# Held VectorE operations, and softmax weights turned on VectorE and through DRAM, in a one-layer hybrid decoder step

## The chip, the cores and the metric

The kernel runs on one core of a Trainium2 chip. The metric is the device time of one execution in microseconds; the time given is the median of three executions. The profile is of one further execution.

## The reference, cut to what matters

One decoder layer with three branches that read the same normalised input, for a prompt of 1024 tokens and for 8 sample tokens that share the weights:

```
h = rmsnorm(x);  q, k, v, gla_g, a_lr, u, pool_g, xq, xg, merge = split(h @ w_in)
br_gla  = rmsnorm(gla_chunked(q, k, v, log_sigmoid(a_lr @ w_a2 + b_a)/16, S0)) * silu(gla_g)
br_pool = multiscale_pool(u, hist) * silu(pool_g)
s = einsum('bthd,bmhd->bhtm', xq, mem_k) * 256 ** -0.5      # 4 heads of 256, 256 memory rows
c = einsum('bhtm,bmhd->bthd', softmax(s), mem_v)
br_x = c * silu(xg)
y = x + (sum over n of sigmoid(merge_n) * (branch_n @ w_branch_n)) @ w_out, then rmsnorm
```

The sample tokens run the same layer, each against its own cached memory keys and values. All is float32 (the matmuls in three products of split operands, see below), D_MODEL is 1024.

## The kernel before, in words

**Products.** The input projection is worked off in 36 `Pair`s of column blocks, each by a scheme of seven products instead of eight (`product`, `half`-wise). An operand is split into a high part, written by ScalarE, and a remainder, written by VectorE (`split`, L220 and L221; scaled, L223 and L224), and each product is three matmuls (`mm3`, L239 to L241): high by high, high by remainder, remainder by high. The operand sums of a pair (`of`, L300) are made by VectorE on the raw block that a DMA loaded; names are a11, a12, a22 (blocks) and s1 to s4 (sums, in the two `ws` tiles); the sums of product results are the `c` rows (L676, L693, L702) with the `r` that ScalarE saved (L611). Operands are prepared three products ahead.

**Side streams.** After each half product, `fill()` lets the other work advance, in amounts that constants and the costs yielded by each stream decide: the memory's keys and values, cross attention, GLA, pooling. TensorE, SyncE (SP) and the loads stand in written order. The order on VectorE, ScalarE and GpSimd is made by a scheduler; `tc.issue_after(x)` keeps an operation from standing earlier than x on its engine.

**Cross attention** (`cross_steps`). 4 heads by 4 chunks of 256 tokens make 16 steps. Step s runs scores(s), queries(s+1), the load of xq(s+2), a step of the sample tokens, values(s-2), another sample step, at the head's end the next head's memory, weights(s-1), and three more sample steps.

- `cross_scores`: 12 matmuls into a PSUM bank `pz`, maxima (nm, L766), exponentials (L75), reciprocal and scaling (L771, L773), giving p with tokens on partitions.
- `cross_weights`: four 128x128 transposes on TensorE (L781) into another `pz` bank, and the split of that bank into pTh and pTl.
- `cross_values`: 24 matmuls of the values by pT into `pz`, copied out to xo.
- `cross_sample`: for each head, 16 products with reduction on VectorE (L825, two for each of 8 sample tokens, of a key tile kc with a broadcast query qb) write the 16 columns of sc; two TensorE transposes (L835) read all of sc; then maxima (L837), the exponentials and the values.

There are two `pz` banks for all of this. Temporaries come from a ring of 14 tiles; key tiles from four others; qb from two tags of two buffers, which the gate's tiles use later. Queries, keys and pT are loaded by SP, which works in order.

**Elsewhere.** GLA's `states` scale and update the sample tokens' states, ScalarE and VectorE (L1098 on); `gate_work` stages the forget gate's loads and weights; `smask` is the mask that resets a scan (L979) every 64 tokens.

Of the kernel before, what the change touches and what calls it, by code (L numbers as in the profile page):

```python
# [18 lines left out]
P = 128  # L19
# [14 lines left out]
CT = 256  # L34
GATE = 16
NE = 30
NR = 14
WORK_A, WORK_B = 497.6, 108.0
WINDOWS = (2, 4, 8, 16)
HIST = 15  # L40
# [7 lines left out]
def trunk_kernel(ctx: ExitStack, tc: tile.TileContext,  # L48
# [81 lines left out]
    def Q(name):  # L130
        return wk.tile([P, QT], F32, tag="q", name=name, bufs=5)

    def tiny(w, name="t", bufs=8):
        return wk.tile([P, 16], F32, tag="t", name=name, bufs=bufs)[:, :w]


    ident = cp.tile([P, P], F32, name="ident")
    make_identity(nc, ident)

    smask = cp.tile([P, CT], BF16, name="smask")  # L140
    nc.gpsimd.memset(smask, 1.0)
    nc.gpsimd.memset(smask.rearrange("p (c t) -> p c t", t=64)[:, :, 0:1], 0.0)
    epst = cp.tile([P, 4], F32, name="epst")
    nc.gpsimd.memset(epst[:, 1:2], 1.0)
    nc.gpsimd.memset(epst[:, 2:3], -0.5 * math.log(DK))
# [38 lines left out]
    ssq = cp.tile([P, 16], F32, name="ssq")  # L184
    nc.vector.memset(ssq, 1.0)

    smp = cp.tile([P, 33 * NS], F32, name="smp")
    brs = [cp.tile([P, NK, NS], F32, name=f"brs{n}") for n in range(3)]
    als = cp.tile([P, NS], F32, name="als")
    als_parts = cp.tile([P, NS], F32R, name="alsp")  # L190
# [7 lines left out]

    PAIR = (P, 4, HT)
    xq_scr, v_scr = scratch(NH, "xqs", (NS, 256)), scratch(NH, "vs", (NS, 256))  # L200
    acc_scr = [scratch(NK, f"acc{n}_", (P, TT)) for n in range(2)]
    mkv_scr = [scratch(NH, f"mkvs{o}", (P, 2, DV)) for o in range(2)]
    al_scr = scratch(2, "als", (P, HT))
# [13 lines left out]
    def split(dst_hi, dst_lo, src, scale=None):  # L217

        if scale is None:
            last["hi"] = nc.scalar.activation(dst_hi, src, AF.Copy)  # L220
            last["lo"] = nc.vector.tensor_tensor(dst_lo, src, dst_hi.bitcast(F32), op=ALU.subtract)  # L221
        else:
            nc.scalar.activation(dst_hi, src, AF.Copy, scale=scale)  # L223
            nc.vector.scalar_tensor_tensor(dst_lo, src, scale, dst_hi.bitcast(F32), op0=ALU.mult, op1=ALU.subtract)  # L224

    def split_r(src, shape, name, scale=None):
        hi, lo = R(shape, F32R, name + "h"), R(shape, F32R, name + "l")
# [54 lines left out]
    class Pair:  # L282
# [11 lines left out]
        def operands(self):  # L294
            lo, hi = self.raw
            a11, a12, a21, a22 = lo[:, :, :P], hi[:, :, :P], lo[:, :, P:], hi[:, :, P:]

            def of(x, y, op, s=None):
                s = wk.tile([P, 4, P], F32, tag="ws", name="ws", bufs=2) if s is None else s
                nc.vector.tensor_tensor(s, x, y, op=op)  # L300
                return s

            def parts(src, name):
                h, l = W2(name + "h"), W2(name + "l")
                split(h, l, src)
                return h, l

            yield parts(a11, "a11")
            yield parts(a12, "a12")
            s1 = of(a21, a22, ALU.add)  # L310
            s2 = of(s1, a11, ALU.subtract)
            yield parts(s2, "s2")
            yield parts(s1, "s1")
            yield parts(of(a11, a21, ALU.subtract), "s3")
            yield parts(of(a12, s2, ALU.subtract, s2), "s4")
            yield parts(a22, "a22")
# [71 lines left out]
        return raw  # L388

    def W2S(dt):  # L390
        return wk.tile([P, 2, P], dt, tag="w2s", name="w2s", bufs=2)

    gate = {}

    def gate_loads():
        for i in range(2):
            gate["w", i] = W2S(F32)
            for j in range(8):
                nc.gpsimd.dma_start(out=gate["w", i][16 * j:16 * j + GATE],
                                    in_=w_a2[:, i * CT:(i + 1) * CT].rearrange("r (h n) -> r h n", h=2))  # L400
# [32 lines left out]
    def gate_work(n):  # L433
        if n == 1:
            gate_loads()
        elif n == 3:
            gate_inputs_load(0)
        elif n == 5:
            gate_weights()
        elif n == 8:  # L440
            gate_inputs(0)
        elif n == 10:
            gate_inputs_load(1)
        elif n == 12:
            gate_inputs(1)

    def mem_units():
# [309 lines left out]
    def cross_scores(h, c):  # L757
        xh, xl = cross["q", h, c]
        mh, ml = cross["mk", h]
        t = PZ()  # L760
        for j in range(2):
            for i in range(2):
                cs = slice(j * P, (j + 1) * P)
                mm3(t[:, j * NM:(j + 1) * NM], xh[:, i, cs], xl[:, i, cs], mh[:, i], ml[:, i], i == 0, i == 1)
        nm = tiny(2, "nm")
        nc.vector.tensor_reduce(nm, t.rearrange("p (j m) -> p j m", j=2), axis=AX.X, op=ALU.max, negate=True)  # L766
        p = R([2, NM], name="p")
        sm = tiny(2, "sm")
        for j in range(2):
            act(p[:, j], t[:, j * NM:(j + 1) * NM], AF.Exp, bias=nm[:, j:j + 1], accum_out=sm[:, j:j + 1])  # L770
        nc.vector.reciprocal(sm, sm)  # L771
        for j in range(2):
            nc.vector.tensor_scalar(p[:, j], p[:, j], sm[:, j:j + 1], None, op0=ALU.mult)  # L773
        cross["p", h, c] = p

    def cross_weights(h, c):
        p = cross["p", h, c]
        t = PZ()
        for a in range(2):
            for j in range(2):  # L780
                nc.tensor.transpose(t[:, (2 * a + j) * P:(2 * a + j + 1) * P], p[:, j, a * P:(a + 1) * P], ident)  # L781
        cross["pT", h, c] = split_r(t.rearrange("p (a t) -> p a t", a=2), [2, CT], "pT")

    def cross_values(h, c):
        ph, pl_ = cross["pT", h, c]
        vh, vl = cross["mv", h]
        g = R([2, CT], name="xo")
        t = PZ()
        for i in range(2):
            cs = slice(i * P, (i + 1) * P)  # L790
            for a in range(2):
                mm3(t[:, i * CT:(i + 1) * CT], vh[:, a, cs], vl[:, a, cs], ph[:, a], pl_[:, a], a == 0, a == 1)
        nc.scalar.activation(g, t.rearrange("p (i t) -> p i t", i=2), AF.Copy)
        nc.gpsimd.dma_start(out=mix_chunk(2, h, c), in_=g)

# [22 lines left out]
    def cross_sample(h):  # L818

        sc = wk.tile([P, 16], F32, tag="sc", name="sc", bufs=2)  # L820
        for b in range(NS):
            kcs, qb = cross["kc", h, b // 2]
            kc = kcs[b % 2]
            for a in range(2):
                nc.vector.tensor_tensor_reduce(kc[:, a, :], kc[:, a, :], qb[b % 2],  # L825
                                               scale=1.0, scalar=0.0, op0=ALU.mult, op1=ALU.add,
                                               accum_out=sc[:, a * NS + b:a * NS + b + 1])
            if b in (1, 3):
                cross_keys(h, b // 2 + 2)
            yield 0.7 if b < 7 else 1.2  # L830
            if b == 3:
                yield 0.5
# [55 lines left out]
    def cross_steps():  # L888
        def scores(n):
            cross_scores(n // 4, n % 4)  # L890

        def memory(n):
            if n % 4 == 0:
                cross_memory(n // 4)

        def weights(n):
            cross_weights(n // 4, n % 4)

        def values(n):
# [12 lines left out]
        cross_queries(0, 1)  # L912
        yield 2.5
        for s in range(16 + 2):
            if s < 16:
                scores(s)
                yield 3
                if 0 < s < 15:
                    cross_queries(*divmod(s + 1, 4))
                if s + 2 < 16:  # L920
                    cross_fetch(*divmod(s + 2, 4))
            if s % 4 == 2 and s < 14:
                cross_load(s // 4 + 1)
            if s == 0:
                cross_keys(0, 0)
                cross_keys(0, 1)
            if s >= 1:
                yield next(samples, 0)
            if 0 <= s - 2:
                values(s - 2)  # L930
                yield 1.7
            if s >= 1:
                yield next(samples, 0)
            if s % 4 == 3 and s < 15:
                memory(s + 1)
# [140 lines left out]
    def gla_sample(h):  # L1076
# [21 lines left out]
        def states(b0, s0, vb):  # L1098
            for i in range(2):
                b = b0 + i  # L1100
                nc.scalar.activation(s0[:, i], s0[:, i], AF.Copy, scale=dec[:, b:b + 1])
                nc.vector.scalar_tensor_tensor(s0[:, i], vb[:, i], ks[:, b:b + 1], s0[:, i], op0=ALU.mult, op1=ALU.add)
            nc.gpsimd.dma_start(out=o_gla_s[b0:b0 + 2, h].rearrange("b k v -> k b v"), in_=s0)
            return s0

# [531 lines left out]
```

## Time and profile before

| what | value |
|---|---|
| median of three executions | 1428.67 us (1428.36 to 1433.1) |
| the profiled execution's own time | 1431.94 us |
| its span | 1429.8 us |
| granted TensorE clock | 0.998 |
| TensorE busy | 1410.1 us, 99% |
| VectorE busy | 912.3 us, 64% |
| ScalarE busy | 682.3 us, 48% |
| GpSimd busy | 259.8 us, 18% |

The page has busy time, share of the span and instructions for each engine. Windows give the same for a stretch. A row of the timeline has the start, the length, the engine, the line, the operation, output and inputs, shapes, and in brackets the idle time of the engine ahead of it with what ended it. The waits view sums these by waiting line and by the work waited for: total, times, longest. Cross attention lies between about 100 and 376 us.

### The profile page before, as it was taken

Reading aid. Unit: us, or ns where it says so; the run is one execution under the profiler, and the core shown is the slowest. Engines: PE = TensorE matmul, PEld = TensorE weight load, DVE = VectorE, ACT = ScalarE, POOL = GpSimd, SP = SyncE. Lnnn points to the kernel's source line nnn. Section 1 sums busy time; section 2 is a strip of 40 time slices with the busy share of each in tenths; the row PEclk is TensorE's granted clock in tenths of the full one; section 3 lists DMA queues with packets and bytes.
Section 4 is the critical chain, followed back from the end, with each engine's and each line's share of the span. In section 5 each row is a group of like instructions: output and inputs, shape, how many; then the busy total and the mean of one; then the engine's idle time right before and its main releaser. Section 6 shows DMA issues by size and latency. Waiting matters only on the chain.

```text
span 1429.8 us, 28336 instructions
## 1 busy us (share of the span) xinstructions
PE 1410.1 (99%) x10689; PEld 1352.0 (95%) x10689; DVE 912.3 (64%) x2092; ACT 682.3 (48%) x1582; POOL 259.8 (18%) x465
## 2 busy tenths in 40 slices
PE   7999999999999999999999999999999999999998
PEld 6889999989999999999999999999999999999876
DVE  6956665667687777767765777876662534654336
ACT  6744444444565666656654545444471422333222
POOL 4252111125442232222221111110000000000000
PEclk9999999999999999999999999999999999999999
DMA  9367675666665555555544556566484687632633
GB/s 336 125 204 244 199 244 163 216 186 169 162 183 155 175 175 146 177 156 164 169 142 153 175 154 200 167 206 202 143 276 146 227 272 250 213 104 87 222 117 115
DMA packets 187797, 261.67 MB, mean 183 GB/s; under 512 B 22972, under 2 KB 138708, under 8 KB 187652
## 3 DMA queue, kind: packets, MB, share of 16 engines
q1 hardware_dynamic: 125340, 147.16, 33.3%
q0 software_dynamic: 24160, 74.74, 15.2%
q10 hardware_dynamic: 38160, 37.95, 9.5%
q8 instruction: 84, 1.38, 0.4%
q14 instruction: 53, 0.43, 0.1%
HBM read 181.65 MB, written 78.61 MB: 182 GB/s over the span
## 4 chain that ended last, share of the span: by engine, by line
PE 90%; DMA 5%; DVE 3%; ACT 1%; issue 1%; POOL 1%; SPq 0%; DVEq 0%; ACTq 0%; POOLq 0%
PE px L239 26%; PE px L240 26%; PE px L241 26%; PE pz L240 2%; PE pz L239 2%; PE pz L241 2%; DMA raw<-in_w_in_dram 2%; DMA qb<-xqs 1%; PE pz L1033 1%; PE pz L1012 1%; DMA wm<-in_w_mv_dram 1%; PE pz L862 1%; PE pz L1014 1%; DVE ot L221 0%; DMA wm<-in_w_mk_dram 0%
## 5 line engine op out<-in xcount | busy, mean ns | idle before, releaser
L241 PE MATMUL px<-bh,wbl 128*128 128x384 f32 (+1 forms) x576 | 184.1, 320 | 0.0
L240 PE MATMUL px<-bl,wbh 128*128 128x384 f32 (+1 forms) x576 | 184.1, 320 | 0.0
L239 PE MATMUL px<-bh,wbh 128*128 128x384 f32 (+1 forms) x576 | 183.7, 319 | 0.0
L611 ACT ACTIVATE r<-px 128x258 f32<-128x258 f32 x240 | 90.6, 378 | 58.3 <-PE px L241 57.2
L239 PEld LDWEIGHTS px<-bh,wbh 128*128 128x128 f32 x576 | 108.3, 188 | 0.0
L240 PEld LDWEIGHTS px<-bl,wbh 128*128 128x128 f32 x576 | 108.2, 188 | 0.0
L241 PEld LDWEIGHTS px<-bh,wbl 128*128 128x128 f32 x576 | 108.2, 188 | 0.0
L239 PE MATMUL px<-ot,s1h 128*128 128x258 f32 x320 | 93.3, 292 | 0.0
L239 PE MATMUL px<-o,a11h 128*128 128x258 f32 x320 | 92.8, 290 | 0.0
L239 PE MATMUL px<-o,s4h 128*128 128x258 f32 x320 | 92.5, 289 | 0.3 <-DVE c L693 0.3
L239 PE MATMUL px<-ot,a22h 128*128 128x258 f32 x320 | 92.5, 289 | 0.0
L239 PE MATMUL px<-ot,s2h 128*128 128x258 f32 x320 | 92.4, 289 | 0.0
L239 PE MATMUL px<-ot,s3h 128*128 128x258 f32 x320 | 92.4, 289 | 0.0
L239 PE MATMUL px<-o,a12h 128*128 128x258 f32 x320 | 92.3, 288 | 0.0
L240 PE MATMUL px<-o,a11h 128*128 128x258 f32 x320 | 91.1, 285 | 0.3 <-DVE o L221 0.3
L241 PE MATMUL px<-o,s4l 128*128 128x258 f32 x320 | 90.7, 283 | 0.0
L240 PE MATMUL px<-ot,s2h 128*128 128x258 f32 x320 | 90.1, 282 | 0.5 <-DVE ot L221 0.5
L240 PE MATMUL px<-o,s4h 128*128 128x258 f32 x320 | 90.6, 283 | 0.0
L241 PE MATMUL px<-o,a11l 128*128 128x258 f32 x320 | 90.6, 283 | 0.0
L240 PE MATMUL px<-ot,a22h 128*128 128x258 f32 x320 | 90.6, 283 | 0.0
L241 PE MATMUL px<-o,a12l 128*128 128x258 f32 x320 | 90.4, 283 | 0.0
L241 PE MATMUL px<-ot,s3l 128*128 128x258 f32 x320 | 90.4, 283 | 0.0
(479 smaller groups left out, 4661.4 us busy)
## 6 DMA issues: line engine op xcount, KB each, us to landing
raw<-in_w_in_dram ACTq DMA_DIRECT2D x72, 512.0 KB, 4.1
msc<-c POOLq DMA_DIRECT2D x24, 516.0 KB, 4.9
brsc<-c POOLq DMA_DIRECT2D x24, 516.0 KB, 4.0
sig<-msc SPq DMA_DIRECT2D x24, 516.0 KB, 6.1
brr<-brsc SPq DMA_DIRECT2D x48, 256.0 KB, 5.0
wbr<-in_w_branch_dram SPq DMA_DIRECT2D x24, 512.0 KB, 5.6
acc<-sig POOLq DMA_DIRECT2D x16, 516.0 KB, 5.3
acc<-acc SPq DMA_DIRECT2D x16, 516.0 KB, 7.1
```

The source lines that it names most:

```text
L239: nc.tensor.matmul(out, lhsT=lh, rhs=rh, start=start, stop=False, skip_group_check=more)
L240: nc.tensor.matmul(out, lhsT=lh, rhs=rl, start=False, stop=False, skip_group_check=more)
L241: nc.tensor.matmul(out, lhsT=ll, rhs=rh, start=False, stop=stop, skip_group_check=more)
L611: nc.scalar.activation(r, acc[c][:, :QT], AF.Copy)
L862: nc.tensor.matmul(t[32 * j:32 * j + 32, :DV], lhsT=pm[:, a, 4 * i + j, :], rhs=vc[j][:, a, :], start=a == 0, stop=a == 1)
L1012: nc.tensor.matmul(t[0:64, 0:P], lhsT=ki[:, 0:64], rhs=qi, start=True, stop=True)
L1014: nc.tensor.transpose(t[:, P:2 * P], kt, ident)
L1033: nc.tensor.matmul(to, lhsT=kiqi[:, 1, cs], rhs=st, start=False, stop=True)
```

## The change

**Holds.** Four kinds of operation are placed no earlier than something else on their engine. `of`'s sums stand behind the last remainder that `split` wrote (`last["lo"]`). The sample scores' products stand behind the last maxima of the scores and behind the last remainder. GLA's state updates, and the split of the turned weights, stand behind the last high part and the last remainder; the scaled form of `split` now counts as well.

**Turned weights.** p is turned in blocks of 32x32 by one VectorE instruction, written to DRAM by four GpSimd DMAs of 64 KB, and loaded again by one SP DMA of 256 KB as pT (`cross_turned`, issued in step s for chunk s-1, after xq(s+2)). The split then works on the loaded tile, in place. The 64 transposes on TensorE and their PSUM bank are gone. The values' matmuls read the loaded tile through a view (j, q, c) in runs of 32 elements, and write PSUM in one run.

**Room.** The ring has 15 tiles; tiny tiles 7 for 8; smask is U8 instead of bf16; smp has 32 slots; the W2S tile has one buffer; the gate's raw tile uses tag st; the calls of `gate_work` move.

```diff
-NR = 14
+NR = 15
...
             def of(x, y, op, s=None):
                 s = wk.tile([P, 4, P], F32, tag="ws", name="ws", bufs=2) if s is None else s
-                nc.vector.tensor_tensor(s, x, y, op=op)
+                with tc.issue_after(last["lo"].ins):
+                    nc.vector.tensor_tensor(s, x, y, op=op)
...
-        nc.vector.tensor_reduce(nm, t.rearrange("p (j m) -> p j m", j=2), axis=AX.X, op=ALU.max, negate=True)
+        last["nm"] = nc.vector.tensor_reduce(nm, t.rearrange("p (j m) -> p j m", j=2), axis=AX.X, op=ALU.max, negate=True)
...
-        cross["p", h, c] = p
+        pt = R([512], name="pt")
+        nc.vector.transpose(pt.rearrange("p (b j c) -> p j b c", j=2, c=32), p.rearrange("p j (b c) -> p j b c", c=32))
+        for q in range(4):
+            nc.gpsimd.dma_start(out=pt_scr[4 * h + c][:, :, q, :].rearrange("b r x -> r b x"),
+                                in_=pt[32 * q:32 * q + 32].rearrange("r (b x) -> r b x", b=8))
 
     def cross_weights(h, c):
-        p = cross["p", h, c]
-        t = PZ()
-        for a in range(2):
-            for j in range(2):
-                nc.tensor.transpose(t[:, (2 * a + j) * P:(2 * a + j + 1) * P], p[:, j, a * P:(a + 1) * P], ident)
-        cross["pT", h, c] = split_r(t.rearrange("p (a t) -> p a t", a=2), [2, CT], "pT")
+        with tc.issue_after(last["hi"].ins), tc.issue_after(last["lo"].ins):
+            cross["pT", h, c] = split_in(cross["pr", h, c], [2, CT], "pT")
+
+    def cross_turned(h, c):
+        cross["pr", h, c] = loaded(pt_scr[4 * h + c].rearrange("(a b) r q x -> (b r) a (q x)", a=2), [2, CT], "pT")
...
-                mm3(t[:, i * CT:(i + 1) * CT], vh[:, a, cs], vl[:, a, cs], ph[:, a], pl_[:, a], a == 0, a == 1)
+                rh, rl = (x[:, a].rearrange("p (q j c) -> p j q c", q=4, j=2) for x in (ph, pl_))
+                mm3(t[:, i * CT:(i + 1) * CT].rearrange("p (j q c) -> p j q c", j=2, q=4), vh[:, a, cs], vl[:, a, cs],
+                    rh, rl, a == 0, a == 1)
...
-            for a in range(2):
-                nc.vector.tensor_tensor_reduce(kc[:, a, :], kc[:, a, :], qb[b % 2],
+            with tc.issue_after(last["nm"].ins), tc.issue_after(last["lo"].ins):
+                for a in range(2):
+                    nc.vector.tensor_tensor_reduce(kc[:, a, :], kc[:, a, :], qb[b % 2],
...
+            if 0 <= s - 1 < 16:
+                cross_turned(*divmod(s - 1, 4))
...
-                nc.scalar.activation(s0[:, i], s0[:, i], AF.Copy, scale=dec[:, b:b + 1])
-                nc.vector.scalar_tensor_tensor(s0[:, i], vb[:, i], ks[:, b:b + 1], s0[:, i], op0=ALU.mult, op1=ALU.add)
+                with tc.issue_after(last["hi"].ins), tc.issue_after(last["lo"].ins):
+                    nc.scalar.activation(s0[:, i], s0[:, i], AF.Copy, scale=dec[:, b:b + 1])
+                    nc.vector.scalar_tensor_tensor(s0[:, i], vb[:, i], ks[:, b:b + 1], s0[:, i], op0=ALU.mult, op1=ALU.add)
```

The order on TensorE at the first chunk's weights, before (rows with buffer numbers; an ot is an activation block, s3h and s3l an operand):

```order
L239 MATMUL px_1449<-ot310_814,s3h_1582 128x258
L240 MATMUL px_1449<-ot311_815,s3h_1582 128x258
L241 MATMUL px_1449<-ot310_814,s3l_1583 128x258
L781 MATMUL pz_1779<-ident_72,p_1632 128x128 x4
L239 MATMUL px_1450<-ot300_809,s3h_1582 128x258
L240 MATMUL px_1450<-ot301_810,s3h_1582 128x258
```

The same place now (line numbers of the changed kernel, one or more higher):

```order
L240 MATMUL px_1465<-ot310_830,s3h_1598 128x258
L241 MATMUL px_1465<-ot311_831,s3h_1598 128x258
L242 MATMUL px_1465<-ot310_830,s3l_1599 128x258
L240 MATMUL px_1466<-ot300_825,s3h_1598 128x258
L241 MATMUL px_1466<-ot301_826,s3h_1598 128x258
L242 MATMUL px_1466<-ot300_825,s3l_1599 128x258
```

Sixteen such rows of four transposes are gone from TensorE, and no other of its rows has moved.

VectorE ahead of the sample scores' transposes of head 0, before: the last products (ISA; kc a key tile, sc the scores), and what follows them. The maxima nm that read the transposes' bank stand five rows further on.

```order
L825 ISA kc_1833,sc_1747<-kc_1833,qb_1836 128x256
L825 ISA sc_1747 128x1
L771 RECIPROCAL sm_1855<-sm_1855 128x2
L773 TENSOR_SCALAR p_1854<-p_1854,sm_1855 128x256 x2
L221 TENSOR_TENSOR s2l_1880<-ws_1877,s2h_1879 128x512
L702 TENSOR_TENSOR c2_1883<-px_1716,r2_1655 128x258
L224 SCALAR_TENSOR_TENSOR xq_1745<-xq_1745,xqsh_1897 128x512
L300 TENSOR_TENSOR ws_1877<-raw_1586,ws_1877 128x512
L702 TENSOR_TENSOR c2_1883<-px_1717,r2_1669 128x258
L221 TENSOR_TENSOR s1l_1938<-ws_1875,s1h_1937 128x512
L300 TENSOR_TENSOR ws_1980<-raw_1393 128x512
L221 TENSOR_TENSOR pTl_1962<-pz_1956,pTh_1961 128x512
```

The same place now, up to the last product; nm stands three rows further on:

```order
L678 TENSOR_TENSOR c1_2016<-px_2014,r1_1851 128x258
L222 TENSOR_TENSOR pT_1936<-pT_1936,pTh_1988 128x512
L302 TENSOR_TENSOR ws_2006<-raw_1409 128x512
L678 TENSOR_TENSOR c1_2016<-px_2015,r1_1903 128x258
L222 TENSOR_TENSOR s3l_2009<-ws_2006,s3h_2008 128x512
L833 ISA kc_1855,sc_1777<-kc_1855,qb_1859 128x256
L833 ISA sc_1777 128x1
L833 ISA kc_1855,sc_1777<-kc_1855,qb_1859 128x256
L833 ISA sc_1777 128x1
L833 ISA kc_1857,sc_1777<-kc_1857,qb_1860 128x256
L833 ISA sc_1777 128x1
L833 ISA kc_1857,sc_1777<-kc_1857,qb_1860 128x256
```

The last four products have moved from ahead of the reciprocal to behind the split of pT, the sum ws and two sums c. On TensorE, px_2015 is the half product that stands directly ahead of the transposes of sc:

```order
L240 MATMUL px_2015<-o2110_514,a12h_1831 128x258
L241 MATMUL px_2015<-o2111_515,a12h_1831 128x258
L242 MATMUL px_2015<-o2110_514,a12l_1832 128x258
L843 MATMUL pz_2047<-ident_72,sc_1777 8x128 x2
L240 MATMUL px_1837<-ot200_718,s2h_1909 128x258
```

At head 1 the c that stands ahead of the last six products reads a half product whose last row is 27 TensorE rows ahead of the transposes; between it and the last product stand two products, the splits of pT and of a11, and four products. At head 3 the last c ahead of the last products reads an r that ScalarE saves, and between stand products, a stream transpose and a split.

More of the change, by code (lines that the diff above doesn't have):

```diff
@@ L131, in Q, with tiny @@
         return wk.tile([P, QT], F32, tag="q", name=name, bufs=5)
-    def tiny(w, name="t", bufs=8):
+    def tiny(w, name="t", bufs=7):
         return wk.tile([P, 16], F32, tag="t", name=name, bufs=bufs)[:, :w]
@@ L138, in trunk_kernel @@
     make_identity(nc, ident)
-    smask = cp.tile([P, CT], BF16, name="smask")
-    nc.gpsimd.memset(smask, 1.0)
-    nc.gpsimd.memset(smask.rearrange("p (c t) -> p c t", t=64)[:, :, 0:1], 0.0)
+    smask = cp.tile([P, CT], U8, name="smask")
+    nc.gpsimd.memset(smask, 1)
+    nc.gpsimd.memset(smask.rearrange("p (c t) -> p c t", t=64)[:, :, 0:1], 0)
     epst = cp.tile([P, 4], F32, name="epst")
@@ L185, in trunk_kernel @@
     nc.vector.memset(ssq, 1.0)
-    smp = cp.tile([P, 33 * NS], F32, name="smp")
+    smp = cp.tile([P, 32 * NS], F32, name="smp")
     brs = [cp.tile([P, NK, NS], F32, name=f"brs{n}") for n in range(3)]
@@ L200, in trunk_kernel @@
     xq_scr, v_scr = scratch(NH, "xqs", (NS, 256)), scratch(NH, "vs", (NS, 256))
+    pt_scr = scratch(4 * NH, "pts", (8, 32, 4, 64))
     acc_scr = [scratch(NK, f"acc{n}_", (P, TT)) for n in range(2)]
@@ L222, in split @@
         else:
-            nc.scalar.activation(dst_hi, src, AF.Copy, scale=scale)
-            nc.vector.scalar_tensor_tensor(dst_lo, src, scale, dst_hi.bitcast(F32), op0=ALU.mult, op1=ALU.subtract)
+            last["hi"] = nc.scalar.activation(dst_hi, src, AF.Copy, scale=scale)
+            last["lo"] = nc.vector.scalar_tensor_tensor(dst_lo, src, scale, dst_hi.bitcast(F32), op0=ALU.mult, op1=ALU.subtract)
     def split_r(src, shape, name, scale=None):
@@ L390, in W2S @@
     def W2S(dt):
-        return wk.tile([P, 2, P], dt, tag="w2s", name="w2s", bufs=2)
+        return wk.tile([P, 2, P], dt, tag="w2s", name="w2s", bufs=1)
     gate = {}
@@ L396, in gate_loads @@
         for i in range(2):
-            gate["w", i] = W2S(F32)
+            gate["w", i] = wk.tile([P, CT], F32, tag="st", name="w2r", bufs=2).rearrange("p (h n) -> p h n", h=2)
             for j in range(8):
@@ L435, in gate_work @@
             gate_loads()
-        elif n == 3:
+        elif n == 4:
+            gate_weights()
+        elif n == 7:
             gate_inputs_load(0)
-        elif n == 5:
-            gate_weights()
-        elif n == 8:
+        elif n == 9:
             gate_inputs(0)
-        elif n == 10:
+        elif n == 11:
             gate_inputs_load(1)
-        elif n == 12:
+        elif n == 13:
             gate_inputs(1)
@@ L823, in cross_sample @@
             kc = kcs[b % 2]
-            for a in range(2):
-                nc.vector.tensor_tensor_reduce(kc[:, a, :], kc[:, a, :], qb[b % 2],
-                                               scale=1.0, scalar=0.0, op0=ALU.mult, op1=ALU.add,
-                                               accum_out=sc[:, a * NS + b:a * NS + b + 1])
+            with tc.issue_after(last["nm"].ins), tc.issue_after(last["lo"].ins):
+                for a in range(2):
+                    nc.vector.tensor_tensor_reduce(kc[:, a, :], kc[:, a, :], qb[b % 2],
+                                                   scale=1.0, scalar=0.0, op0=ALU.mult, op1=ALU.add,
+                                                   accum_out=sc[:, a * NS + b:a * NS + b + 1])
             if b in (1, 3):
```

## The prediction

> **What bounds the kernel now.** I read the page first, then the windows by stage, then PE's waits, the chain and the timeline at the waits. On the page, engine busy time:
>
> ```profile
> span 1429.8 us, 28336 instructions
> PE 1410.1 (99%) x10689; PEld 1352.0 (95%) x10689; DVE 912.3 (64%) x2092; ACT 682.3 (48%) x1582; POOL 259.8 (18%) x465
> ```
>
> TensorE is busy for all but 19.9 us, its rows stand in written order, and so the end moves by the matmul time that is taken out and by the time that TensorE is made to wait or is spared. The windows (length, busy time of each engine, clock) say where the change can act; cross attention lies in 100 to 376:
>
> ```profile
> 100.00:376.00 276.00, 272.80 (x2288) 264.21 (x2288) 176.12 (x440) 124.90 (x298) 63.87 (x107) 0.99 0.66 199
> 376.00:400.00 24.00, 23.00 (x193) 21.87 (x192) 20.53 (x56) 15.65 (x40) 12.22 (x21) 1.00 0.57 159
> 400.00:1300.00 900.00, 899.71 (x7000) 884.20 (x6999) 584.26 (x1338) 446.79 (x1047) 141.04 (x245) 1.00 0.57 178
> ```
>
> After 400 TensorE idles 0.3 us in 900: nothing can be saved there, and the GLA states that are now held have only new waits to bring. Before 400 the waits of TensorE are these:
>
> ```profile
> PE pz L373 <- DMA memx<-in_mem_prompt_dram: 5.5, 2, 4.8
> PE pz L239 <- DVE pTl L221: 3.1, 2, 2.0
> PE pz L577 <- ACT mkv L469: 1.3, 1, 1.3
> PE pz L1071 <- DVE ak L221: 1.0, 1, 1.0
> ```
>
> The first and third lie in the start, which the change leaves alone. The second is the scores' matmul waiting for a PSUM bank until VectorE has split the transposed softmax weights out of it. The timeline shows why VectorE was late at the first of the two, and then come the two waits themselves:
>
> ```profile
> 212.16 0.69 DVE L300 TENSOR_TENSOR ws<-raw 128x512 f32<-128x512 f32 x1 [4.59 <-DMA raw<-in_w_in_dram]
> 212.76 0.42 DVE L676 TENSOR_TENSOR c<-px,r 128x258 f32<-128x258 f32 x1
> 213.70 0.69 DVE L221 TENSOR_TENSOR pTl<-pz,pTh 128x512 fp32r<-128x512 f32 x1
> ```
>
> ```profile
> 214.44 0.39 PE L239 MATMUL pz<-mkTh,xqsh 128*128 128x256 f32 x1 [1.01 <-DVE pTl L221]
> 313.63 0.39 PE L239 MATMUL pz<-mkTh,xqsh 128*128 128x256 f32 x1 [2.05 <-DVE pTl L221]
> ```
>
> An operand sum stood 4.59 us in VectorE's queue for its raw load, with everything else behind it. Head-of-queue waits of this kind in that window (VectorE's waits: total, times, longest):
>
> ```profile
> DVE kc L825 <- DMA qb<-xqs: 15.3, 12, 2.5
> DVE ws L300 <- DMA raw<-in_w_in_dram: 11.0, 6, 4.6
> ```
>
> **The change, part by part.** *The transposes go.* The chain (start, length, what) has one group of four between products:
>
> ```profile
> 134.20 0.12 PE px L241
> 134.32 0.44 PE pz L781 x4
> 134.76 0.12 PE px L239
> ```
>
> ```profile
> L781 PE MATMUL pz<-ident,p 128*128 128x128 f32 x64 | 9.6, 272 | 0.0
> ```
>
> 64 in groups of four are 16 groups, and 16 x 0.44 = 7.0 us leave an engine that has nothing else to wait for. The row's 272 ns is a pipelined duration, not spacing. [...] I take 7.0.
>
> *The two pTl waits go*, 3.1 us: no PSUM bank waits for that split any more, and the split reads a loaded tile. The 1.0 us for ak goes if the sum ahead of it (L300) stands later; bounds 0 and 1.0, I take 1.0. Together **-11.1 us**.
>
> *The detour that replaces the transposes*: one stream transpose, four 64 KB stores from GpSimd, one 256 KB load. Rows of the same shapes elsewhere in this kernel:
>
> ```profile
> L1062 DVE STREAM_TRANSPOSE go<-on 128x512 f32<-128x512 f32 x16 | 11.3, 704 | 0.6 <-ACT on L1051 0.6
> L1064 POOL DMA_DIRECT2D onsc<-go x64: 585/588/638, 411.5 to 732.2; - x64
> onsc<-go POOLq DMA_DIRECT2D x64, 64.0 KB, 3.0
> mix<-onsc SPq DMA_DIRECT2D x16, 256.0 KB, 2.9
> ```
>
> 0.70 + 4 x 0.59 + 3.0 + 2.9 = 9.0 us a chunk. VectorE pays 16 x 0.70 = 11.2 us (176.1 of 276 busy there), GpSimd 64 x 0.59 = 37.6 us (63.9 of 276). The cover, for chunk 2: its weights are scaled at the first row, and its transposes stood on TensorE at the second.
>
> ```profile
> 146.45 0.62 DVE L773 TENSOR_SCALAR p<-p,sm 128x256 f32<-128x256 f32 x2
> L781 PE MATMUL pz<-ident,p x4: 270/272/273, 163.7 to 164.0; 128*128 128x128 f32 x4
> ```
>
> 163.7 - 147.1 = 16.6 us for 9.0 of detour, so 7.6 spare. Only chunk 0 is tight: its load stands on SP ahead of key loads and holds them; bounds 0 and 2 us, I take **+0.5**. [...]
>
> *The held products: a new wait.* VectorE's 16 products of sample scores (L825) each head now stand behind the last scores' reduction and the last split. Who waits: TensorE's transposes of the sample scores (L835), once a head, with all products queued behind them. For head 0, before (VectorE's last product; the two sums c; TensorE):
>
> ```profile
> 145.91 0.42 DVE L825 CUSTOM_DVE_ANT_0 kc<-kc,qb 128x256 f32<-128x256 f32 x1
> 151.63 0.69 DVE L221 TENSOR_TENSOR s3l<-ws,s3h 128x512 fp32r<-128x512 f32 x1 [0.16 <-ACT s3h L220]
> 152.49 0.75 DVE L676 TENSOR_TENSOR c<-px,r 128x258 f32<-128x258 f32 x2
> ```
>
> ```profile
> 151.03 0.28 PE L241 MATMUL px<-o,a12l 128*128 128x258 f32 x1
> 151.15 0.38 PE L835 MATMUL pz<-ident,sc 128*8 128x128 f32 x2
> ```
>
> The products were done 4.8 us early. In the new order, the last four stand behind a c that reads the half product (px_2015) ending in TensorE's row just ahead of the transposes. So at best c starts some 0.2 us after TensorE is ready (end of the matmul's 0.28 less the 0.12 spacing), and then come c 0.35, s3l 0.6, four products at 0.35 and a read 0.08 (spacings from the rows): 0.2 + 0.35 + 0.6 + 1.4 + 0.08, near 2.7; with a semaphore, **2.8 us**. It is more if pT's split, ahead of that c, is late. Heads 1 and 3, from these rows:
>
> ```profile
> 208.44 0.63 ACT L220 ACTIVATE a11h<-raw 128x512 fp32r<-128x512 f32 x1 [1.25 <-issue]
> 211.62 0.38 PE L835 MATMUL pz<-ident,sc 128*8 128x128 f32 x2
> ```
>
> ```profile
> 338.36 0.37 ACT L611 ACTIVATE r<-px 128x258 f32<-128x258 f32 x1
> 339.14 0.38 PE L835 MATMUL pz<-ident,sc 128*8 128x128 f32 x2
> ```
>
> Head 1: the c that the new order puts there reads a half product that ends 27 TensorE rows ahead of the transposes, 27 x 0.12 = 3.2 us, at 208.4; then c 0.35, two products 0.7, two splits 1.2, four products 1.5 and latencies near 0.3 end at 212.5: **1.0 us**. Head 3: c waits for ACT's r until 338.7; then c 0.35, four products 1.5, a stream transpose 0.6, a split 0.6, latencies 0.3 end at 341.9 less the 0.35 of a product that may slip ahead, 341.5: **2.4 us**. Head 2 has no such c behind its last split; I take **0.3**. Sum **+6.5 us**. Bounds: 0, if ready work stood idle in my count, and 12, about twice it, if pT's split is late each time.
>
> *Without a term*: the ring of 15, the U8 mask (its scan, 0.68 us, runs where VectorE has slack), the gate's moved loads, W2S with one buffer: each off TensorE's path, and by the windows TensorE waits 1.0 us in all where they act.
>
> **The sum.** -11.1 + 6.5 + 0.5 = -4.1 us. The profiled execution took 1431.94 us (span 1429.8 and 2.1 around it), 3.3 above the median of 1428.67, so it would come to 1427.8; taken from the median, **1424.6 us**.
>
> **The rivals.** *Holds free* (0.25): the products run before they are needed, waits of 0 to 2 us. For it: VectorE is 36% idle, and the sum that blocked it for 4.59 us is moved. Against: c's place above. Then -11.1 + 0.5 + 0 to 2, some -9.6: 1417 to 1420.5, middle 1419.
>
> *Holds give nothing back* (0.18): the wait for raw loads only moves, and scores then wait 3 to 4 us elsewhere for banks. For it: six waits at L300 in that window, of which only one cost TensorE. Then -7.0 + 6.5 + 0.5 = 0, up to +3: 1428.7 to 1432.
>
> *Slower: the strided moving operand* (0.08). The values' matmuls now read the weights in runs of 32 elements a row. No row of before reads so. The nearest slow form is plain fp32 against fp32r of the same size:
>
> ```profile
> L460 PE MATMUL pz<-wm,memT 128*128 128x256 f32 x128 | 30.2, 390 | 0.0
> L239 PE MATMUL pz<-pTh,mvsh 128*128 128x256 f32 x64 | 18.1, 282 | 0.0
> ```
>
> 3 x 64 = 192 matmuls by 390 - 282 = 108 ns are 20.7 us as a ceiling; nothing excludes it, and below nothing it can't go, as the bytes are the same. With it, -4.1 + 20.7: 1445. It decides from 4.1 / 192 = 21 ns apiece. I take 0: the output stays contiguous. [...] No run shows it yet.
>
> *SP behind the key loads* (0.06): key tiles come free later since their products are held, and SP, in order, holds the queries' and pT's loads behind them. It decides beyond the 7.6 us to spare; at 4 us beyond, once a head, 16 us: 1441.
>
> **How the numbers follow.** The forecast, 0.43, spans 1421 to 1428. About 0.5% (7.1 us: 1421.5 and 1435.8) is what a measurement can tell from no change. Faster: all of holds free and 0.13 of the forecast, 0.38. Slower: the last two and 0.01 of the waits' upper bound, 0.15. Within: 0.47. The range 1416.5 to 1434 leaves out most of the last two, and holds both bounds of the waits: 1424.6 - 6.5 less the chunk-0 term and a little, and + 5.5, with the third case's upper end.
>
> **What would show it.** Right: no transposes at the weights; no pTl among TensorE's waits; TensorE waiting at the sample scores' transposes for sc, some 2.8, 1.0, 0.3 and 2.4 us; the values' matmuls at 0.12 us spacing. Wrong: that wait missing (then 1419), a wait for pT or xq, a spacing above 0.14 us, or pTl's wait come back under another name at the scores.

## The result, and the profile after

The changed kernel takes 1455.97 us (median of four, 1453.47 to 1457.09), the kernel before beside it 1430.64 us. The ratio is 1.0174, with a 95% interval of 1.0159 to 1.0189: 25 us slower, where 4 us less were forecast and 1434 was the range's upper end.

The page of the changed kernel, its span and the busy time of each engine:

```profile
span 1454.2 us, 28368 instructions
PE 1413.2 (97%) x10625; PEld 1353.5 (93%) x10625; DVE 923.9 (64%) x2108; ACT 684.2 (47%) x1582; POOL 296.9 (20%) x529
```

The span grew by 24.4 us. TensorE's idle time went from 19.7 to 41.0 us, so 21.3 of it is waiting. The other 3.1 is busy time, and that with 64 matmuls less: as these stood for 7.0 us by the prediction's price, the rest of the work took 10.1 us longer. Most of both sits in cross attention, as the window shows (length, busy times, granted clock, DMA share and GB/s): TensorE idles there for 20.3 us, where it idled for 3.2. Another 2.8 us of waiting came in the start and 1.7 at the last chunk, just behind this window; after 400 nothing changed:

```profile
100.00:376.00 276.00, 255.70 (x2062) 247.27 (x2065) 174.34 (x436) 116.44 (x278) 90.58 (x157) 0.94 0.69 217
400.00:1300.00 900.00, 899.88 (x7043) 883.12 (x7042) 596.55 (x1375) 455.32 (x1078) 153.94 (x264) 1.00 0.58 180
```

TensorE's waits in the changed kernel (total, times, longest) name the place:

```profile
PE pz L843 <- DVE sc L833: 20.3, 4, 7.5
...
PE pz L240 <- ACT wmsh L221: 2.2, 1, 2.2
PE pz L240 <- ACT pTh L221: 1.9, 1, 1.9
...
PE pz L241 <- DVE wmsl L222: 1.5, 2, 1.3
PE pz L241 <- DVE pT L222: 0.8, 1, 0.8
```

The waits for pTl and ak are gone, as forecast. The transposes of the sample scores wait for the held products, as forecast, once a head, but 20.3 us and not 6.5. The rows for wms lie in the start and those for pT at the last chunk; neither had a term.

How head 0 came to wait 7.5 us is read backwards over four timelines of the changed kernel. TensorE, and VectorE's split and last product:

```profile
162.03 0.63 PE L843 MATMUL pz<-ident,sc 128*8 128x128 f32 x2 [7.48 <-DVE sc L833]
```

```profile
158.17 0.69 DVE L222 TENSOR_TENSOR pT<-pT,pTh 128x512 fp32r<-128x512 f32 x1 [4.53 <-ACT pTh L221]
161.81 0.42 DVE L833 CUSTOM_DVE_ANT_0 kc<-kc,qb 128x256 f32<-128x256 f32 x1
```

The split of pT, ahead of the last four products, stood 4.53 us at the head of VectorE's queue for ScalarE's high part, and that stood for the load:

```profile
157.51 0.63 ACT L221 ACTIVATE pTh<-pT 128x512 fp32r<-128x512 f32 x1 [5.39 <-DMA pT<-pts]
```

And the load had been issued at 150.93, behind a pair of key loads that SP could not finish issuing for 4.42 us. ScalarE could start on it 6.6 us after its issue, while key, query and memory loads were on their way with it (the median of these pT loads is 4.5 us in this kernel; the prediction took 2.9 from a row of before):

```profile
141.06 0.37 SPq L729 DMA_DIRECT2D pT<-pts  x1
141.52 0.93 SPq L729 DMA_DIRECT2D kc<-in_cache_mem_k_dram  x2
142.51 0.93 SPq L822 DMA_DIRECT2D qb<-xqs  x2
143.54 4.42 SPq L729 DMA_DIRECT2D kc<-in_cache_mem_k_dram  x2
...
150.93 0.37 SPq L729 DMA_DIRECT2D pT<-pts  x1
```

SP's own waits over cross attention say for what: mostly for tiles that are free when the held products have read them.

```profile
SPq L729 <- DVE sc L833: 58.0, 24, 8.5
```

In the kernel before this row was 11.3 us:

```profile
SPq L727 <- DVE sc L825: 11.3, 10, 5.0
```

For the pair at 143.54 itself the view names the sum c (L704, 3.4 us) that stands right behind two products; by time it is these products, at 146.78 and 147.12, after which SP issued the second load at 147.6. They stood behind the split of the first chunk's pT, which had itself waited 1.71 us for its load.

So the profile suggests a circle: held products free key tiles late, key loads hold SP, SP holds pT's load, and the next held products stand behind pT's split. The experiments test it. The other 10.1 us are seen in windows behind the wait (busy TensorE time and matmuls, then the granted clock):

```profile
155.00:162.00 7.00, 0.00 (x0) 0.66 0.88 305
162.00:165.00 3.00, 2.97 (x14) 0.50 0.72 236
165.00:170.00 5.00, 5.00 (x35) 0.76 0.15 45
170.00:175.00 5.00, 5.00 (x42) 1.00 0.39 112
```

14 matmuls in 3 us, where at 1.00 there are 42 in 5: behind this wait of 7.48 us TensorE worked at a granted clock of 0.50 until some 5 us after the wait's end, and from 167.5 at 1.00 (by half-microsecond windows).

### The profile page after: what moved, and what is told of

Read it like the earlier page. It is cut to its first block, busy times and chain, and to the rows that moved or that the text cites. A ratio compares the mean times of both kernels' runs of the same rounds, so it can differ in the third digit from the quotient of the medians.

```text
span 1454.2 us, 28368 instructions
## 1 busy us (share of the span) xinstructions
PE 1413.2 (97%) x10625; PEld 1353.5 (93%) x10625; DVE 923.9 (64%) x2108; ACT 684.2 (47%) x1582; POOL 296.9 (20%) x529
## 4 chain that ended last, share of the span: by engine, by line
PE 91%; DMA 4%; DVE 3%; ACT 1%; issue 1%; SPq 0%; POOL 0%; DVEq 0%; ACTq 0%
PE px L240 26%; PE px L241 26%; PE px L242 26%; PE pz L241 3%; PE pz L242 2%; PE pz L240 2%; DMA raw<-in_w_in_dram 1%; DMA pT<-pts 1%; PE pz L1043 1%; PE pz L1022 1%; DMA wm<-in_w_mv_dram 1%; DVE kc L833 1%; PE pz L1024 1%; PE pz L870 1%; DMA vc<-in_cache_mem_v_dram 0%
## 5 line engine op out<-in xcount | busy, mean ns | idle before, releaser
L240 PE MATMUL px<-ot,s1h 128*128 128x258 f32 x320 | 93.9, 293 | 0.0
L240 PE MATMUL px<-ot,s3h 128*128 128x258 f32 x320 | 93.1, 291 | 0.0
L240 PE MATMUL px<-o,s4h 128*128 128x258 f32 x320 | 92.2, 288 | 0.1
L240 PE MATMUL px<-ot,a22h 128*128 128x258 f32 x320 | 92.1, 288 | 0.0
L241 PE MATMUL px<-ot,s3h 128*128 128x258 f32 x320 | 91.2, 285 | 0.0
L241 PE MATMUL px<-ot,s1h 128*128 128x258 f32 x320 | 90.9, 284 | 0.0
L242 PE MATMUL px<-ot,s1l 128*128 128x258 f32 x320 | 90.9, 284 | 0.0
L242 PE MATMUL px<-ot,s2l 128*128 128x258 f32 x320 | 90.7, 284 | 0.0
```

The costliest lines, as they stand in the source:

```text
L240: nc.tensor.matmul(out, lhsT=lh, rhs=rh, start=start, stop=False, skip_group_check=more)
L241: nc.tensor.matmul(out, lhsT=lh, rhs=rl, start=False, stop=False, skip_group_check=more)
L242: nc.tensor.matmul(out, lhsT=ll, rhs=rh, start=False, stop=stop, skip_group_check=more)
```

## The experiments

Each ratio is to the kernel before on the same chip, with its 95% interval; the medians of before were 1431.66 for the first four, 1430.58 for the next four, 1431.61 for the next three and 1429.94 for the last.

| run | median us | ratio | interval |
|---|---|---|---|
| e1_free_products | 1428.15 | 0.9976 | 0.9967 to 0.9985 |
| e2_pe_transposes | 1434.95 | 1.0016 | 1.0006 to 1.0027 |
| e4_behind_nm | 1428.67 | 0.9982 | 0.9970 to 0.9994 |
| e3_no_holds | 1429.38 | 0.9992 | 0.9979 to 1.0004 |
| e5_own_queue | 1479.28 | 1.0338 | 1.0321 to 1.0356 |
| e6_sums_from_pair4 | 1422.35 | 0.9944 | 0.9930 to 0.9959 |
| e7_last_chunk | 1418.51 | 0.9915 | 0.9900 to 0.9930 |
| e8_sums_only | 1432.42 | 1.0007 | 0.9997 to 1.0017 |
| e9_chunk_behind | 1457.20 | 1.0184 | 1.0151 to 1.0217 |
| e10_free_sums | 1425.52 | 0.9949 | 0.9929 to 0.9970 |
| e11_sums_alone_late | 1425.85 | 0.9958 | 0.9944 to 0.9972 |
| e12_load_first | 1446.86 | 1.0113 | 1.0096 to 1.0130 |

### Which part costs: four kernels

**e1_free_products** takes the hold off the products.

```diff
-            with tc.issue_after(last["nm"].ins), tc.issue_after(last["lo"].ins):
-                for a in range(2):
-                    nc.vector.tensor_tensor_reduce(kc[:, a, :], kc[:, a, :], qb[b % 2],
+            for a in range(2):
+                nc.vector.tensor_tensor_reduce(kc[:, a, :], kc[:, a, :], qb[b % 2],
```

> The changed kernel without the hold on the sample scores' products; everything else as changed. Theory A (hold and detour together: the last products stand behind the split of pT, which waits on ScalarE for a load that came through DRAM, so TensorE waits 20.3 us at the sample scores' transposes, and after each wait its clock is lower): those waits fall to under 2 us in all, and the time comes to 1418 to 1424 us. Theory B (the detour is late in itself: pT's high part blocks ScalarE, and the queues behind it, whatever stands there): TensorE waits 10 us or more at other places in the same stretch, and the time stays above 1438 us. Theory C (the strided reads of the values cost): above 1440 us with slower matmuls at the values.

The wait at the sample scores is gone. What is left in its waits view beside the load at the start:

```profile
PE pz L240 <- ACT wmsh L221: 2.1, 1, 2.1
PE pz L240 <- ACT pTh L221: 1.9, 1, 1.9
PE pz L241 <- DVE wmsl L222: 1.3, 1, 1.3
...
PE pz L241 <- DVE pT L222: 0.8, 1, 0.8
```

The span is 1426.7 us, 27.5 below the changed kernel's, for one edit: 20.3 us of waits, and TensorE's same 10,625 matmuls take 1405.9 us busy instead of 1413.2, which is the clock (worked out below). SP's waits for the products fall from 58.0 to 5.0 us. Theory B falls, as the detour does no such harm alone, and so does theory C. But theory A expected 1418 to 1424 and got 1428.15: something else costs 4 us or more. The rows above say where to look.

**e2_pe_transposes** keeps every hold and goes back to transposes on TensorE.

```diff
-        with tc.issue_after(last["hi"].ins), tc.issue_after(last["lo"].ins):
-            cross["pT", h, c] = split_in(cross["pr", h, c], [2, CT], "pT")
+        p = cross["p", h, c]
+        t = PZ()
+        for a in range(2):
+            for j in range(2):
+                nc.tensor.transpose(t[:, (2 * a + j) * P:(2 * a + j + 1) * P], p[:, j, a * P:(a + 1) * P], ident)
+        with tc.issue_after(last["hi"].ins), tc.issue_after(last["lo"].ins):
+            cross["pT", h, c] = split_r(t.rearrange("p (a t) -> p a t", a=2), [2, CT], "pT")
```

> The changed kernel with the weights transposed on TensorE again and split out of PSUM; all holds stay, that on the products too. Theory A: the split no longer waits for a load, so only the hold's own price is left, waits at the sample scores' transposes of 2.8 us for head 0 and some 6 us for all four, and with the transposes' 7 us back the time comes to 1432 to 1438 us. Theory B: the same place, as the detour is gone: 1428 to 1434 us. A hold that is costly without the detour (theory D) would leave 12 us of waits or more, 1445 us and above.

```profile
PE pz L842 <- DVE sc L832: 2.3, 2, 1.8
```

The time is within theory A's 1432 to 1438, the waits are under its 6 us (0.6 at head 0, 1.8 at head 3). The hold without the detour costs 2.3 us of waits; the detour without the hold costs none at this place; both together cost 20.3. Neither part is the cause alone, and a sum of prices could not give this. Theory D falls. SP stands for the held products here nearly as long as in the changed kernel:

```profile
SPq L729 <- DVE sc L832: 55.9, 24, 8.0
```

So the hold alone stops SP, with 2.3 us of harm to TensorE as long as nothing that the products stand behind comes by that queue.

**e4_behind_nm** leaves the products behind the scores' maxima and drops the second condition.

```diff
-            with tc.issue_after(last["nm"].ins), tc.issue_after(last["lo"].ins):
+            with tc.issue_after(last["nm"].ins):
```

> The changed kernel with the products held behind the scores' maxima only, no longer behind the last split. Theory A: as without the hold, 1418 to 1424 us, waits at the sample scores' transposes under 2 us in all, since no product stands behind pT's split any more. Theory D (any hold of the products is costly, as they come later and bunched): waits of 5 us or more stay, 1428 us or more. Theory B: above 1438 us.

No wait for sc is among its waits, and the ratio, 0.9982, agrees with that of e1 within the intervals. It is the place behind the last remainder that matters, as theory A has it: the last four products of head 0 run at 152.6 to 154.0, ahead of the second chunk's split of pT. The time misses its 1418 to 1424 by 4.7 us, about as e1 does.

**e3_no_holds** frees all four kinds of operation, among them:

```diff
-                with tc.issue_after(last["lo"].ins):
-                    nc.vector.tensor_tensor(s, x, y, op=op)
+                nc.vector.tensor_tensor(s, x, y, op=op)
```

> The turned weights without any of the holds (operand sums, products, GLA states, the split of the turned weights all free). Theory A, in which the detour is covered by itself: 1418 to 1426 us; the difference from the kernel without the products' hold is what the hold of the operand sums is worth, which I put at 0 to 3 us in favour of holding. Theory B: above 1438 us.

0.9992: turning the weights without any hold is no gain that can be told from none, and above theory A's 1418 to 1426. Against e1 the hold of the sums (with those of the split and of the states) would be worth 2.3 us by ratio, but the intervals overlap. The waits show that it acts both ways: the two for wms, 3.4 us in e1, are down to 0.4, but TensorE idles 5.7 us in the window of cross attention, against 3.3 in e1.

### The missing 4 us: sums and the last chunk

**e6_sums_from_pair4** is e1 with the operand sums held from the fifth pair on only.

```diff
+        p_.held = i >= 4
...
+                if self.held:
+                    with tc.issue_after(last["lo"].ins):
+                        nc.vector.tensor_tensor(s, x, y, op=op)
+                else:
+                    nc.vector.tensor_tensor(s, x, y, op=op)
```

> The changed kernel without the products' hold, and with the hold on the operand sums only from the fifth pair on. The hold is read as costing at the start, where the raw loads of the first pairs and the memory's weights share the sums' buffers and queues: two waits of TensorE for wms of 1.3 and 2.1 us against 0.4 before, and 53 rows against 65 in the 10 us behind them. If so, the start is as before, and the time is 3 to 5 us below that of the kernel without the products' hold: 1422 to 1426 us. If the lower rate there has another cause: the same within 1.5 us, some 1428 us.

0.9944 against 0.9976: the hold in the start cost some 4.6 us, and both waits for wms above 1 us are gone. The time is as expected, and the views show the way, which is the one of head 0 again. In e1 a held sum runs at 62.78, in the kernel before at 45.10 and in e6 at 44.77. Until it has read its raw tile SP stands at a raw load, and the loads of wms behind that are issued from 63.94, not 36.55 (e6: 36.26):

```profile
SPq L292 <- DVE ws L302: 30.1, 1, 30.1
```

ScalarE then stands 2.21 us for a late load of wms, TensorE waits, and its clock is 0.85 in 70 to 80 us.

**e7_last_chunk** adds transposes on TensorE for the last of the 16 chunks.

```diff
+        if (h, c) == (NH - 1, 3):
+            cross["p", h, c] = p
+            return
         pt = R([512], name="pt")
```

> As the kernel before it in this list, with the last of the 16 chunks transposed on TensorE again. The two waits of 1.9 and 0.8 us for pT at the last chunk, where too little work is left to cover the round trip, go for 0.44 us of transposes: 1.5 to 3 us less than without this edit, 1420 to 1424 us. If something else is late there, the difference is under 1 us.

0.9915, 4 us better than e6 by ratio and below its expected band by 1.5 us. The waits account for half of that: TensorE idles 2.0 us less than in e6, and its busy time is 2.0 us less, four transposes included. In e6 its clock was halved behind these two waits:

```profile
360.00:363.00 3.00, 3.00 (x16) 0.51 0.69 188
```

With the waits for pTh and pT gone, TensorE waits for nothing between 100 and 376 us:

```profile
100.00:376.00 276.00, 276.00 (x2327) 267.06 (x2326) 192.64 (x485) 130.77 (x317) 105.47 (x178) 1.00 0.74 233
```

This is the fastest version: 12 us under the kernel before.

**e8_sums_only** is the kernel before with the hold on the sums alone, from the first pair.

```diff
-                nc.vector.tensor_tensor(s, x, y, op=op)
+                with tc.issue_after(last["lo"].ins):
+                    nc.vector.tensor_tensor(s, x, y, op=op)
```

> The kernel before with the hold on the operand sums alone. By the prediction's second term the two waits for pTl and the one for ak go, 4.1 us; by the reading of the start the hold costs 3 to 5 us there. Both together: 1428 to 1433 us, no measurable difference, with pTl gone from TensorE's waits and wms new among them. If the pTl waits stay, the hold did not remove them, and the time is 1433 to 1436 us.

1.0007, no difference, with the expected exchange in its waits: pTl and ak gone, and new

```profile
PE pz L239 <- ACT wmsh L220: 2.6, 1, 2.6
```

**e11_sums_alone_late** is the same with `p_.held = i >= 4`, as in e6.

> The kernel before with the operand sums held from the fifth pair on, and nothing else. If the hold removes the two waits for pTl and the one for ak without the turned weights, the time is 3 to 5 us below the kernel before, 1425 to 1428 us by its median of 1430.6, and what the turned weights give beside it is their 7 us of transposes. If those waits need the turned weights: no measurable difference, and the turned weights are worth some 11 us.

0.9958, some 6 us, and 276.00 of 276 us busy in the window of cross attention. So the hold on the sums removes the pTl waits with the transposes still on TensorE; the prediction gave that to the freed PSUM bank. Of the 6.2 us in the span 3.7 are idle time, as the prediction has it, and 2.5 are busy time.

**e10_free_sums** is e7 without that hold.

```diff
-        p_.held = i >= 4
+        p_.held = False
```

> The fastest version so far (turned weights but for the last chunk, products free, sums held from the fifth pair on) with the operand sums free throughout. If the hold on the sums is worth what its theory says (no raw load ahead of VectorE's queue in cross attention), TensorE's waits there come back by 2 to 5 us, 1420 to 1424 us. If the turned weights alone do it, since no PSUM bank waits for their split any more: the same within 1.5 us, 1417 to 1420 us.

0.9949: the hold is worth 4.9 us to e7. Without it, a new wait stands in the same stretch:

```profile
PE pz L879 <- DVE ps L868: 6.0, 2, 3.2
```

and VectorE stands again for raw loads, which in e7 is not among its waits there:

```profile
DVE ws L305 <- DMA raw<-in_w_in_dram: 15.6, 5, 6.7
```

The time is some 1.5 us above the 1420 to 1424 of the first reading. The second reading falls: the turned weights alone don't free VectorE's queue.

### Is it the circle? Three kernels

**e5_own_queue** loads pT from GpSimd's queue, right behind its stores, with all holds kept.

```diff
+        pr = R([2, CT], name="pT")
+        nc.gpsimd.dma_start(out=pr, in_=pt_scr[4 * h + c].rearrange("(a b) r q x -> (b r) a (q x)", a=2))
+        cross["pr", h, c] = pr
...
-            if 0 <= s - 1 < 16:
-                cross_turned(*divmod(s - 1, 4))
```

> The changed kernel, all holds kept, with pT loaded from GpSimd's queue right behind its stores and no longer from SP's. Theory A1 (the circle on SP: pT's load stands behind key loads that wait for key tiles, which the held products free late): pT is there early, the waits at the sample scores' transposes fall from 20.3 us to the held order's own price, 4 to 8 us, and the time to 1431 to 1440 us. Theory A2 (the round trip through DRAM is itself too long for the place of the split): the waits stay at 12 us or more, and the time above 1445 us.

1479 us: slower still, and inconclusive. In head 0 pT was split early enough (its high part at 141.85), but another thing came late in its place: SP stood 11.5 us at a load of qb, VectorE 4.34 us at a product for that qb, and the wait at the sample scores was 24.4 us in all.

```profile
PE pz L846 <- DVE sc L836: 24.4, 4, 7.4
PE pz L242 <- DVE xq L225: 10.4, 5, 7.8
```

A1's number is missed and A2's met, yet not for A2's reason; the run tells the two apart no better than before.

**e9_chunk_behind** loads, for each chunk, what the chunk before it had stored; the values are computed from another chunk's weights.

```diff
+        src = [pt_scr[max(n - k, 0)].rearrange("(a b) r q x -> (b r) a (q x)", a=2) for k in (1, 0)]
...
+            nc.sync.dma_start(out=pr, in_=src[0])
```

> The changed kernel with all its holds, except that each chunk's pT load reads what the chunk before it stored (chunk 0 its own, the last one half of each), so that the values are computed from another chunk's weights; number, size and place of the loads and the order of VectorE up to the last chunk stay. Theory S1 (a load stands on SP until its own store has landed, and that decides): no load but chunk 0's waits for a store, and the waits at the sample scores' transposes fall below 10 us, those of heads 1 to 3 to 6 us in all; time 1433 to 1443 us. Theory S2 (the load is late because SP stands behind key loads whose tiles the held products free late, or takes long to land): the waits stay at 15 us or more, the time at 1448 us or more.

1.0184, as the changed kernel. Its waits of TensorE and of SP:

```profile
PE pz L851 <- DVE sc L841: 20.0, 4, 8.0
```

```profile
SPq L729 <- DVE sc L841: 57.3, 23, 8.8
```

No chunk but the first and the last had its own store to wait for, and nothing became better: S1 falls. It is not the load's wait for its store; how long the load itself takes to land is not tested here.

**e12_load_first** keeps everything and issues each pT load one step earlier, ahead of the key loads.

```diff
-            if 0 <= s - 1 < 16:
-                cross_turned(*divmod(s - 1, 4))
...
                 weights(s - 1)
                 yield 1.7
+            if s < 16:
+                cross_turned(*divmod(s, 4))
```

> The changed kernel with all holds, and pT's load of each chunk issued on SP one step earlier, ahead of the key loads that wait for tiles which the held products free. If SP's queue behind those key loads is what makes pT late (theory S2), ScalarE's waits for pT fall from 22.7 us to under 10, and TensorE's waits at the sample scores' transposes from 20.3 us to the held order's own price, 4 to 9 us; time 1432 to 1442 us. If the load is late for how long it takes to land, or the key loads themselves are late and hold the last products, the waits stay at 14 us or more and the time at 1447 us or more.

ScalarE's waits for pT in that window fall from 22.7 to 2.0 us, and TensorE's at the sample scores to 7.7:

```profile
PE pz L843 <- DVE sc L833: 7.7, 3, 4.2
...
PE pz L861 <- DVE ps L850: 3.2, 1, 3.2
PE pz L242 <- DVE xq L225: 2.6, 1, 2.6
```

```profile
164.19 0.63 PE L843 MATMUL pz<-ident,sc 128*8 128x128 f32 x2 [4.23 <-DVE sc L833]
224.79 0.53 PE L843 MATMUL pz<-ident,sc 128*8 128x128 f32 x2 [0.61 <-DVE sc L833]
346.94 0.53 PE L843 MATMUL pz<-ident,sc 128*8 128x128 f32 x2 [2.84 <-DVE sc L833]
```

4.2, 0.6, none and 2.8 us by head, and S2 holds for the wait. The place on SP and the landing are not wholly parted by this, as a load that is issued a step earlier has more time to land as well. The changed kernel's trace gives a measure: the stores of head 0's second chunk were issued by 140.4 and take 3.7 us to land (median), so its load, issued at 150.93, was some 6 to 7 us later than its data allowed (an estimate), while its 6.6 us of landing are 2.1 above the median. The time, 1446.86, is above S2's 1432 to 1442. TensorE has new waits, for queries (xq, and 1.2 us for xqsh) and at ps, and its clock falls behind four waits of cross attention (of 2.64, 4.23, 2.84 and 3.18 us; the window's mean is 0.98, and matmuls that stand some 0.12 us apart elsewhere stand some 0.21 apart there). Loads that stand early on SP wait there for their stores, and queries and keys stand behind them; that the new waits come from this is read from the view, and no run tests it:

```profile
SPq L729 <- DMA pts<-pt: 84.8, 24, 16.6
```

The links are shown by taking each out (e1 and e4, e2, e12). That the delay also feeds itself round after round is not shown: SP's waits for the products are 55.9 us in e2, where the circle is open, and 58.0 where it is closed.

## Why the prediction was wrong, point by point

**The transposes, -7.0: right.** e7 against e11 differs by them, but for one group, and by the changes of room and the hold of GLA's states: 0.9915 against 0.9958 is 6.2 us, and TensorE's busy time 1401.4 against 1407.6 us is 6.2 as well; 15 groups of 0.44 are 6.6. So by these two runs turning the weights off TensorE pays, where TensorE is 99% busy and the turn is covered.

**The pTl and ak waits, -4.1: right in size, wrong in cause.** The hold on the sums is enough to remove them (e11, 0.9958). Freeing the PSUM bank also takes away the row for pTl (e10), but VectorE still stands for raw loads (15.6 us) and TensorE then waits at ps (6.0 us). The 4.1 was read from waits that did go; as a price it was short, as the clock behind them, 1.7 us in the kernel before, was not in it (e11 gains 6.2 us of span).

**The held products, +6.5: the place was right, and this is the step that failed in size: 20.3.** By head it was 7.48, 6.12, 3.54 and 3.16 us, where 2.8, 1.0, 0.3 and 2.4 were forecast. The price was worked out with pT's split on time, its lateness being left to a bound of 12. By the order alone it was fair: e12, with pT mostly on time, waits 7.7 us in all, and e2, with no load to wait for, 2.3. The rival "SP behind the key loads", at 0.06, named the other half: SP held by key tiles. What the prediction did not do is put the two together. It took 7.6 us to spare for pT from the times of before, in which the products were early, and charged the hold and the detour apart. The detour's own 9.0 us were short as well: by medians its stores took 3.7 us and its loads 4.5, not 3.0 and 2.9. e1, e2 and e4 show that each alone is cheap, e9 that it is not the store, and e12 that it is the load's place on SP, behind loads that the held products stop, that makes them dear together.

**The clock: a term that was missing, 10.1 us.** A wait was charged its own length. In the windows above TensorE runs at 0.50 behind the one of 7.48 us. The size can be worked out from half-microsecond windows: TensorE's busy time in each, times the share of the clock that was not granted. That gives 10.2 us behind the four waits and 1.7 in the start, against 1.7 in the kernel before (behind its wait of 2.05 us): 10.2 more, beside the 10.1 found by subtraction. The same sum is 4.6 in e1, 1.7 in e6, and none in e7, e10 and e11. Without it TensorE's busy time is 1408.4 us in the kernel before and 1401.3 in the changed one, e1 and e7 being within 0.1 of that: the 7.0 of the transposes once more. So the clock accounts for all of this term; its parts are e1 against the changed kernel (7.4 us busy) and e6 against e1 (2.6).

**Chunk 0, +0.5, and "without a term".** Chunk 0's load did hold SP for its store (two waits of 6.0 us in all in the changed kernel's 125 to 165), but TensorE did not wait for it alone. The last chunk had no term and cost 2.7 us of waits, as less work follows it; in e6, where the clock fell behind them, taking them out saved 3.9 us of span (e7). The hold on the sums in the start had none either and cost some 4.6 us (e6 against e1): the prediction looked for its effect in cross attention only.

**The strided operand, 0: right.** The values' matmuls of the changed kernel take what they took before, 283 ns against 282, and stand 0.12 us apart in both:

```profile
L240 PE MATMUL pz<-pTh,mvsh 128*128 128x256 f32 x64 | 18.1, 283 | 1.9 <-ACT pTh L221 1.9
```

No row of the kernel before showed the 0; this row, beside the 282 ns of before, shows it. GLA's held states cost nothing: TensorE idles 0.1 us from 400 to 1300.

**The sum, as measured.** Waits: +20.3 at the sample scores, -4.1 for pTl and ak, +3.3 for wms, +2.7 at the last chunk: 22.2 against the 21.3 of idle time. Work: -7.0 of transposes, +10.1 of clock. The idle time and the work together are the 24.4 us of the span. Of the prediction's own figures, TensorE's idle time was 19.7 us, not 19.9, the terms of head 3 add up to 0.15 us more than stated, and the 0.1 for a semaphore and 0.3 for latencies stand on no row; none of this moves the forecast.

## What to carry to other kernels

Here a hold behind another engine's result tied VectorE's queue to everything that this result waited for: TensorE waited 2.3 us with the hold alone, not at all at that place with the detour alone, and 20.3 us with both. So follow the chain round, loads and the tiles they need included, and see whether it closes, before any price is added to another. The changed kernel's four waits of TensorE, of 3.16 to 7.48 us, cost 10.2 us more than their length, by the clock of 0.50 behind them. A hold that helps in one stage should be confined to it (the hold on the sums cost some 4.6 us in the start), and a covered detour needs its cover in the last iteration too (2.7 us of waits here).

## What was not expected of the hardware

The granted clock fell in each of the four waits of the changed kernel, of 7.48, 6.12, 3.54 and 3.16 us, to 0.50, and was back at 1.00 between 2.8 and 6.1 us after the wait's end (by half-microsecond windows). A shorter wait did it too. In the kernel before, behind the single wait of 2.05 us that ended at 313.63, the clock was at 0.50 from 315.0 to some 318.3:

```profile
316.00:319.00 3.00, 3.00 (x18) 0.60 0.52 139
```

The wait of 1.01 us at 214.44 left the clock at 1.00. Length alone does not decide between these two: the pair of 1.88 and 0.85 us at the last chunk, with a little work between, left the clock at 1.00 in the changed kernel (near 394), and halved it in e6 (the row at 360 above). What decides there is open. Once it fell, these runs lost 1.4 to 3.0 us of TensorE's time behind each wait, by the sum above.
